# MLP up-projection of an encoder trunk: from channel-major matmuls of 512 and 256 columns to token-major matmuls of 512, its output turned on VectorE and GpSimd

## The chip, the cores and the metric

The kernel runs on one core of a Trainium2 chip. A core has TensorE (PE, matrix products into PSUM), ScalarE (ACT), VectorE (DVE), GpSimd (POOL) and SyncE (SP, which issues the weight DMAs here). Each engine takes its own queue of instructions in order. The metric is the time of one execution on the device in microseconds; three executions of the kernel before gave 2285.25, 2285.56 and 2286.99 us.

## The reference

Two layers of an encoder over 256 tokens of width 2048, all in float32. Layer 0 mixes by grouped-query attention, layer 1 by dilated windows; each is followed by a gated MLP with a depthwise convolution of width 3 over the tokens. The change touches the MLP alone:

```python
def rms_norm(x, gain):
    xf = x.astype(jnp.float32)
    y = xf * lax.rsqrt(jnp.mean(xf * xf, axis=-1, keepdims=True) + EPS) * gain.astype(jnp.float32)
    return y.astype(x.dtype)

def conv_ffn(h, w_up, conv_w, conv_b, w_down):
    u = h @ w_up                                  # (256, 2048) @ (2048, 11264)
    c = u.shape[-1]
    pad = CONV_WIDTH // 2
    u = lax.conv_general_dilated(u, conv_w[:, None, :].astype(u.dtype), window_strides=(1,),
                                 padding=((pad, pad),), dimension_numbers=('NWC', 'WIO', 'NWC'),
                                 feature_group_count=c) + conv_b
    gate, val = jnp.split(u, 2, axis=-1)
    return (jax.nn.silu(gate) * val) @ w_down

def reference(x, ...):
    h = x
    for i in range(DEPTH):                        # DEPTH = 2
        hn = rms_norm(h, mix_norm[i])
        ...
        h = h + conv_ffn(rms_norm(h, ffn_norm[i]), w_up[i], conv_w[i], conv_b[i], w_down[i])
    return rms_norm(h, final_norm)
```

## The kernel before

**Products.** A float32 product is made of three: each operand is split into a high part rounded to fp32r and a low rest, and high x high, high x low and low x high are summed in PSUM. The activations are split once per stage. Weights are split as they arrive: SP loads 128 x 1024 values (`raw`), ACT copies them rounded (`wh`, L113 and L165), DVE subtracts (`wl`, L114 and L166). `raw`, `wh` and `wl` have four buffers each (NRAW, NHL), so a new split waits until PE is done with the one four before it. The splits are recorded with a raised priority (AHEAD), so the scheduler puts them ahead of other work of the same engine.

**Token-major and channel-major.** In `feed` and `project` the stationary operand is a block of 128 tokens and the moving one 512 weight columns: two accumulators, one for each block of tokens, hold tokens on partitions and channels along the row (L153 to L155, 24 matmuls of 512 columns for each group of 512 input channels, "k-group"). The mixers' projections, the attention outputs and the down-projection go that way. The up-projection goes through `feed_T` instead: the stationary operand is 128 weight columns, the moving one the tokens, so channels lie on partitions. Its high weights meet high and low activations side by side in one matmul of 2 x 256 columns (L129); its low weights meet the high activations in one of 256 columns (L127). The halves of an accumulator must then be added (L428, L429), and the normalising factor `rstd` of each token, which lies along the row in this layout, is spread over the partitions once per layer by `bcast_rstd` (L375) and multiplied in (L431).

**The MLP.** 11264 columns are 11 gate blocks and 11 value blocks of 512, taken as pairs; pairs 0 to 5 and then 6 to 10 (HALVES). Each half makes its up-projections, and then a down-projection over its share of the hidden channels. Before, a block is taken in two halves of 256 columns (`hh`). The first one of a layer is fed in three parts, because the activations of the last k-group are still being turned and split at that time. `up_post` handles an accumulated half-block: empty it into `u`, make the middle tap and the bias of the convolution on ACT (L433), add the two outer taps on DVE (L438, L440); for the gate Silu on ACT (L443), for the value `glu`: the product on POOL (L448) and its split into `slots` for the down-projection (L242, L243).

**What sets the order.** Such work is written as generators: `start` runs one up to its first `yield`, and each `step`, called between groups of matmuls, runs the oldest one further; `drain` finishes what is left. The scheduler then orders each engine's queue by what its instructions need and by priority. The transposes of the activations between stages (`late_transpose`) already use DVE's blockwise transposes of 32 x 32 (`quad_T`, L288) and POOL copies between partitions (`quad_move`, L292), as does mixer B.

Of the kernel before, what the change touches and what calls it, by code (L numbers as in the profile page):

```python
# [13 lines left out]
P = 128  # L14
D = 2048
NT = 256
# [14 lines left out]
def tile_encoder(ctx: ExitStack, tc: tile.TileContext, x, xT, w_a, w_ao, q_gain, k_gain, w_b, w_bo,  # L31
# [26 lines left out]
    def nm(s):  # L58
        uid[0] += 1
        return f"{s}_{uid[0]}"  # L60
# [38 lines left out]

    def feed_T(acc, lhs, w, n, hh, kgs, first, last):  # L100
        raws = []
        for kg in kgs:
            raw = spool.tile([P, 2, 512], F32, tag="raw", name=nm("raw"), bufs=NRAW)
            raws.append(raw.rearrange("p a c -> p (a c)").rearrange("p (k c) -> p k c", c=NT))
            src = w[n, kg].rearrange("p (k c) -> p k c", c=512)[:, :, hh * NT:(hh + 1) * NT]
            nc.sync.dma_start(raws[-1], src)
        hls = []
        for rk in raws:
            wh = spool.tile([P, 2, 512], F32R, tag="wh", name=nm("wh"), bufs=NHL)
            wl = spool.tile([P, 2, 512], F32R, tag="wl", name=nm("wl"), bufs=NHL)  # L110
            wh, wl = (t.rearrange("p a c -> p (a c)").rearrange("p (k c) -> p k c", c=NT) for t in (wh, wl))
            with tc.high_priority(offset=AHEAD):
                nc.scalar.activation(wh, rk, AF.Copy)  # L113
                nc.vector.tensor_tensor(wl, rk, wh.bitcast(F32), ALU.subtract)  # L114
            hls.append((wh, wl))
        lows = (True, False) if kgs[0] == 2 and len(kgs) == 2 or kgs[0] == 3 else (False, True)
        spent, left, total = 0, len(kgs), 3 * len(kgs) * 8
        for n_run, low in enumerate(lows):
            fin = last and n_run == 1
            order = [(i, kt, j) for i in range(len(kgs)) for kt in range(4) for j in range(2)]  # L120
            for i, kt, j in sorted(order, key=lambda o: o[2]) if fin else order:
                c = slice(j * P, (j + 1) * P)
                st = first and n_run == 0 and i == 0 and kt == 0
                sp = fin and i == len(kgs) - 1 and kt == 3
                x, w2 = lhs[4 * kgs[i] + kt], hls[i]
                if low:
                    nc.tensor.matmul(acc[j][:, :NT], w2[1][:, kt, c], x[0], start=st, stop=sp)  # L127
                else:
                    nc.tensor.matmul(acc[j], w2[0][:, kt, c], x[2], start=st, stop=sp)  # L129
                spent += 1 if low else 2  # L130
                if spent >= total - 24 * (left - 1):
                    left -= 1
                    step()
# [234 lines left out]
    def bcast_rstd(rbc, rstd, pool):  # L368
        yield
        dg = pool.tile([P, 2, P], F32, name=nm("dg"))  # L370
        for m in range(2):
            nc.vector.tensor_scalar(dg[:, m, :], ident, rstd[:, m:m + 1], None, op0=ALU.mult)
        yield
        t = ps_tile()
        nc.tensor.matmul(t[:, :NT], ones, dg.rearrange("p m c -> p (m c)"), start=True, stop=True)  # L375
        nc.vector.tensor_copy(rbc, t[:, :NT])

# [16 lines left out]

    def ffn(l, hT, ss_in, cw, g_next, last, side=None):
        with tc.tile_pool(name=nm("fpool"), bufs=1) as fp:
            junk = junk_of(fp)
            next_space[0] = fp, ("quad", 1), ("tT", 1)
# [22 lines left out]
            def up_post(acc, n, hh, c, after=None):  # L421
                u = us.pop(0)
                us.append(u)
                k0 = 2 * hh
                yield
                v = fp.tile([P, 2, NT], F32, tag="v", name=nm("v"), bufs=2)
                for j in range(2):
                    nc.scalar.activation(v[:, j], acc[j][:, NT:], AF.Copy)  # L428
                    nc.vector.tensor_tensor(v[:, j], acc[j][:, :NT], v[:, j], ALU.add)  # L429
                o = u.rearrange("p j (m t) -> p j m t", m=2)[:, :, :, :P]  # L430
                nc.vector.tensor_tensor(o, v.rearrange("p j (m t) -> p j m t", m=2), rb4, ALU.mult)  # L431
                for j in range(2):
                    nc.scalar.activation(halves(c[:, j]), halves(u[:, j])[:, :, :P], AF.Identity,  # L433
                                         bias=tap(n, k0 + j, 3), scale=tap(n, k0 + j, 1))
                yield
                for j in range(2):
                    cj = halves(c[:, j])
                    nc.vector.scalar_tensor_tensor(cj, halves(u[:, j, :NT])[:, ::-1], tap(n, k0 + j, 0), cj,  # L438
                                                   ALU.mult, ALU.add)
# [626 lines left out]
```

## Time and profile before

| | |
|---|---|
| median of three runs | 2285.56 us |
| profiled execution | 2286.25 us |
| its span, first to last instruction | 2284.4 us |
| mean granted TensorE clock | 0.999 |
| PE / PEld / DVE / ACT / POOL busy | 2271.6 / 1941.1 / 1618.5 / 1199.2 / 202.4 us |
| HBM read | 429.2 MB, 189 GB/s over the span |

The profile shows one execution. Its views, as they are used below: the page gives each engine's busy time and, followed back from the last instruction, the chain of work that ended last; the groups put instructions of one line, engine and shape together, with their count, the time that they cover, the mean ns of one, and the idle time of the engine just before them with what ended it; a source or tile view gives min, median and max of one line's instructions; windows give busy time and counts of each engine in a stretch; the timeline gives instructions in order. Matmuls overlap in their pipeline, so the distance from one to the next is shorter than the length that is recorded for one.

### The profile page before, as it was taken

Reading aid. Unit: us, or ns where it says so; the run is one execution under the profiler, and the core shown is the slowest. Engines: PE = TensorE matmul, PEld = TensorE weight load, DVE = VectorE, ACT = ScalarE, POOL = GpSimd, SP = SyncE. Lnnn points to the kernel's source line nnn. Section 1 sums busy time; section 2 is a strip of 40 time slices with the busy share of each in tenths; the row PEclk is TensorE's granted clock in tenths of the full one; section 3 lists DMA queues with packets and bytes.
Section 4 is the critical chain, followed back from the end, with each engine's and each line's share of the span. In section 5 each row is a group of like instructions: output and inputs, shape, how many; then the busy total and the mean of one; then the engine's idle time right before and its main releaser. Section 6 shows DMA issues by size and latency. Waiting matters only on the chain.

```text
span 2284.4 us, 31068 instructions
## 1 busy us (share of the span) xinstructions
PE 2271.6 (99%) x11589; PEld 1941.1 (85%) x11589; DVE 1618.5 (71%) x2292; ACT 1199.2 (52%) x1755; POOL 202.4 (9%) x233
## 2 busy tenths in 40 slices
PE   9999999999999999999999999999999999999998
PEld 7888888888888888888888888888888888888887
DVE  6877977776457776878876876677777744677755
ACT  7565565554345554555454554446555533555543
POOL 2331100000000000010030003001000000000010
PEclk9999999999999999999999999999999999999999
DMA  8534565566555655576555554566565565555564
GB/s 301 167 131 163 196 192 186 185 195 196 194 190 184 192 189 199 184 217 206 190 178 180 181 186 167 182 199 206 186 194 188 190 196 192 190 189 192 185 199 152
DMA packets 256728, 433.43 MB, mean 190 GB/s; under 512 B 13752, under 2 KB 194744, under 8 KB 256448
## 3 DMA queue, kind: packets, MB, share of 16 engines
q1 hardware_dynamic: 254768, 425.91, 57.0%
q0 software_dynamic: 1520, 5.25, 1.1%
q8 instruction: 90, 1.47, 0.3%
q14 instruction: 62, 0.51, 0.1%
q10 hardware_dynamic: 288, 0.30, 0.0%
HBM read 429.20 MB, written 2.20 MB: 189 GB/s over the span
## 4 chain that ended last, share of the span: by engine, by line
PE 91%; DVE 4%; issue 1%; DMA 1%; ACT 1%; POOL 1%; SPq 0%; DVEq 0%; POOLq 0%; ACTq 0%
PE acc L129 27%; PE acc L154 15%; PE acc L155 15%; PE acc L153 15%; PE acc L127 14%; DVE wl L166 2%; DVE tT L297 2%; DMA raw<-in_w_b_dram 1%; PE ps L258 1%; PE ps L257 0%; PE ps L256 0%; ACT wh L165 0%; POOL wide L292 0%; PE ps L776 0%; PE ps L254 0%
## 5 line engine op out<-in xcount | busy, mean ns | idle before, releaser
L166 DVE TENSOR_TENSOR wl<-raw,wh 128x1024 fp32r<-128x1024 f32 (+1 forms) x452 | 549.9, 1220 | 305.0 <-ACT wh L165 301.5
L165 ACT ACTIVATE wh<-raw 128x1024 fp32r<-128x1024 f32 (+1 forms) x452 | 470.3, 1045 | 495.5 <-PE acc L155 408.2
L129 PE MATMUL acc<-xh,wh 128*128 128x512 f32 x2816 | 657.4, 390 | 1.2 <-DVE v L429 1.2
L129 PEld LDWEIGHTS acc<-xh,wh 128*128 128x128 f32 x2816 | 522.5, 188 | 106.5 <-DVE v L429 1.9
L114 DVE TENSOR_TENSOR wl<-raw,wh 128x1024 fp32r<-128x1024 f32 x352 | 416.7, 1223 | 83.7 <-ACT wh L113 78.1
L113 ACT ACTIVATE wh<-raw 128x1024 fp32r<-128x1024 f32 x352 | 362.8, 1054 | 64.9 <-ACT v L428 30.2
L153 PE MATMUL acc<-wh,ah 128*128 128x512 f32 x1008 | 392.7, 390 | 0.0
L155 PE MATMUL acc<-wh,al 128*128 128x512 f32 x1008 | 392.3, 389 | 0.0
L154 PE MATMUL acc<-wl,ah 128*128 128x512 f32 x1008 | 392.3, 389 | 0.0
L127 PEld LDWEIGHTS acc<-xh,wl 128*128 128x128 f32 x2816 | 350.6, 192 | 7.9 <-ACT wh L113 0.3
L127 PE MATMUL acc<-xh,wl 128*128 128x256 f32 x2816 | 353.2, 283 | 0.0
L153 PE MATMUL acc<-wh,xh 128*128 128x512 f32 x768 | 302.1, 394 | 1.0 <-ACT wh L165 1.0
L154 PE MATMUL acc<-wl,xh 128*128 128x512 f32 x768 | 299.5, 390 | 0.2 <-DVE wl L166 0.2
L155 PE MATMUL acc<-wh,xh 128*128 128x512 f32 x768 | 299.7, 390 | 0.0
L155 PEld LDWEIGHTS acc<-wh,al 128*128 128x128 f32 x1008 | 189.2, 188 | 39.2
L153 PEld LDWEIGHTS acc<-wh,ah 128*128 128x128 f32 x1008 | 189.3, 188 | 38.9
L154 PEld LDWEIGHTS acc<-wl,ah 128*128 128x128 f32 x1008 | 189.2, 188 | 38.9
L155 PEld LDWEIGHTS acc<-wh,xh 128*128 128x128 f32 x768 | 144.1, 188 | 30.6
L153 PEld LDWEIGHTS acc<-wh,xh 128*128 128x128 f32 x768 | 144.4, 188 | 29.1 <-ACT wh L165 1.4
L154 PEld LDWEIGHTS acc<-wl,xh 128*128 128x128 f32 x768 | 144.4, 188 | 28.4 <-DVE wl L166 0.5
L448 POOL TENSOR_TENSOR cv<-cg,cv 128x512 f32<-128x512 f32 x44 | 60.0, 1363 | 1153.6 <-DVE cv L440 1153.6
L242 ACT ACTIVATE ah<-cv 128x256 fp32r<-128x256 f32 x88 | 32.0, 411 | 169.2 <-POOL cv L448 169.2
(179 smaller groups left out, 1508.0 us busy)
## 6 DMA issues: line engine op xcount, KB each, us to landing
raw<-in_w_up_dram SPq DMA_DIRECT2D x352, 512.0 KB, 4.6
raw<-in_w_down_dram SPq DMA_DIRECT2D x176, 512.0 KB, 3.8
raw<-in_w_b_dram SPq DMA_DIRECT2D x144, 512.0 KB, 4.1
raw<-in_w_bo_dram SPq DMA_DIRECT2D x48, 512.0 KB, 3.6
raw<-in_w_a_dram SPq DMA_DIRECT2D x40, 512.0 KB, 4.3
raw<-in_w_ao_dram SPq DMA_DIRECT2D x32, 512.0 KB, 3.6
raw<-in_w_a_dram SPq DMA_DIRECT2D x16, 256.0 KB, 5.8
h<-in_x_dram SPq DMA_DIRECT2D x4, 512.0 KB, 7.8
```

The lines of the kernel that those rows point to most:

```text
L113: nc.scalar.activation(wh, rk, AF.Copy)
L114: nc.vector.tensor_tensor(wl, rk, wh.bitcast(F32), ALU.subtract)
L127: nc.tensor.matmul(acc[j][:, :NT], w2[1][:, kt, c], x[0], start=st, stop=sp)
L129: nc.tensor.matmul(acc[j], w2[0][:, kt, c], x[2], start=st, stop=sp)
L153: nc.tensor.matmul(accs[m], xh[:, c], wh[:, j, :], start=st, stop=False)
L154: nc.tensor.matmul(accs[m], xh[:, c], wl[:, j, :], start=False, stop=False)
L155: nc.tensor.matmul(accs[m], xl[:, c], wh[:, j, :], start=False, stop=sp)
L165: nc.scalar.activation(wh[:, c], r[:, c], AF.Copy)
L166: nc.vector.tensor_tensor(wl[:, c], r[:, c], wh[:, c].bitcast(F32), ALU.subtract)
L242: nc.scalar.activation(hi, src, AF.Copy)
L297: nc.vector.transpose(o[cols].rearrange("p a (m t) -> p a m t", m=2)[:, :, :, rows], s[rows].rearrange("p m (a c) -> p a m c", c=P)[:, :, ...
L448: nc.gpsimd.tensor_tensor(cv, cg, cv, ALU.mult)
```

## The change

The up-projection uses `project` and `project2` as the other projections do, with accumulators of 128 tokens x 512 channels. ACT empties them with `rstd` as the scale of each partition (`evac_scaled`). Then `turned` brings the block to channel-major: two DVE instructions transpose it in 32 x 32 blocks into `quad`, and 16 POOL copies move the blocks to their partitions in `u`, which now holds four groups of 128 channels. The convolution, Silu, product and split work on whole blocks of 512 channels. `feed_T`, `bcast_rstd`, `up_post` and `glu` are gone; new generators spread the work over the feeds, and the outputs of a value block are split while the next pair runs, or, for the last of a half, by `flush` in the down-projection.

```diff
-    def feed_T(acc, lhs, w, n, hh, kgs, first, last):
...
-    def bcast_rstd(rbc, rstd, pool):
...
+    def evac_scaled(pool, accs, rstd, bufs=2):
+        o = pool.tile([P, 2, 512], F32, tag="stg", name=nm("stg"), bufs=bufs)
+        for m in range(2):
+            nc.scalar.activation(o[:, m, :], accs[m], AF.Copy, scale=rstd[:, m:m + 1])
+        return o
...
-            next_space[0] = fp, ("quad", 1), ("tT", 1)
+            next_space[0] = fp, ("quad", 2), ("tT", 1)
...
-            us = [fp.tile([P, 2, 258], F32, name=nm("u")) for _ in range(3)]
+            us = [fp.tile([P, 4, 2, 129], F32, name=nm("u")) for _ in range(3)]
             for u in us:
-                nc.gpsimd.memset(u[:, :, P:P + 1], 0.0)
-            rbc = fp.tile([P, NT], F32, name=nm("rbc"))
-            rb4 = rbc.rearrange("p (m t) -> p m t", m=2)[:, None].to_broadcast([P, 2, 2, P])
-            start(bcast_rstd(rbc, rstd, fp))
+                nc.gpsimd.memset(u[:, :, 0, P:], 0.0)
...
-            def up_post(acc, n, hh, c, after=None):
...
-            def glu(cg, cv, slots, k0):
...
+            def conv(blk):
+                n, u, c = blk
+                for j in range(4):
+                    tc.keep_in_program_order(nc.scalar.activation(
+                        halves(c[:, j]), u[:, j, :, :P], AF.Identity, bias=tap(n, j, 3), scale=tap(n, j, 1)))
+                    if j == 1:
+                        yield
+                flat = u.rearrange("p j m t -> p j (m t)")
+                for j in range(4):
+                    cj = halves(c[:, j])
+                    for i, o in ((0, 0), (2, 1)):
+                        nc.vector.scalar_tensor_tensor(cj, halves(flat[:, j, o:o + NT])[:, ::-1], tap(n, j, i), cj,
+                                                       ALU.mult, ALU.add)
+                    if j == 1:
+                        yield
+
+            def turned(s, u):
+                quad = quad_tile(fp, "quad", 2)
+                for m in range(2):
+                    quad_T(quad, slice(m, 8, 2), s[:, m])
+                for q, c in QC:
+                    nc.gpsimd.tensor_copy(u[32 * c:32 * c + 32, :, :, 32 * q:32 * q + 32],
+                                          quad[32 * q:32 * q + 32, c].rearrange("p (j m) t -> p j m t", m=2))
+
+            def gate_gen(accs, blk, value):
+                s = evac_scaled(fp, accs, rstd, 1)
+                yield
+                if value is None:
+                    turned(s, blk[1])
+                    return
+                yield from product(value)
+                with tc.issue_after(value[4].pop()):
+                    turned(s, blk[1])
+
+            def product(value):
+                n, u, cv, cg, made, _, _ = value
+                yield from conv((n, u, cv))
+                made.append(nc.gpsimd.tensor_tensor(cv, cg, cv, ALU.mult).ins)
+
+            def value_gen(accs, blk, gate, last):
+                s = evac_scaled(fp, accs, rstd, 1)
+                yield
+                turned(s, blk[1])
+                for _ in range(1 if last else 4):
+                    yield
+                yield from conv(gate)
+                nc.scalar.activation(gate[2], gate[2], AF.Silu)
+                if last is not None:
+                    yield
+                    yield from act_split(last)
+
+            def act_split(value):
...
+                    tc.keep_in_program_order(nc.scalar.activation(hi, cv[:, j, :], AF.Copy))
+                    nc.vector.tensor_tensor(lo, cv[:, j, :], hi.bitcast(F32), ALU.subtract)
...
+            def flush(value):
+                yield
+                yield from product(value)
+                yield
+                yield
+                yield from act_split(value)
...
-                    for hh in range(2):
...
+                    if p == 0:
+                        va = project2(w_up[l], 0, NPAIR, hT, kgs, 1, gate_done)
+                    else:
+                        gate_done(project(w_up[l], p, hT, kgs))
+                        va = project(w_up[l], NPAIR + p, hT, kgs)
+                    start(value_gen(va, value, gate, last_value))
+                    last_value = value
...
+                start(flush(last_value))
...
-                drain(1)
```

The order of the instructions moves as follows.

On PE, in the up-projection of layer 0 before the change, at a pair's middle (`xh` are activations, `wl` and `wh` weights, the shape is that of the moving operand):

```order
L127 MATMUL acc_4601<-xh_2757,wl_4671 128x256
L127 MATMUL acc_4602<-xh_2757,wl_4671 128x256
L129 MATMUL acc_4601<-xh_2531,wh_4666 128x512
L129 MATMUL acc_4601<-xh_2534,wh_4666 128x512
L129 MATMUL acc_4601<-xh_2537,wh_4666 128x512
```

And on PE in the changed kernel, at the start of a value block of layer 0:

```order
L118 MATMUL acc_3939<-wh_3945,xh_2285 128x512
L119 MATMUL acc_3939<-wl_3946,xh_2285 128x512
L120 MATMUL acc_3939<-wh_3945,xh_2285 128x512
L118 MATMUL acc_3940<-wh_3945,xh_2285 128x512
L119 MATMUL acc_3940<-wl_3946,xh_2285 128x512
```

The runs of 256 columns are gone; all matmuls have 512, three for each accumulator.

On POOL, at the start of layer 0's MLP before the change (`rb`, `oh`, `rh`, `rl` belong to the bias lines of mixer B):

```order
L808 TENSOR_TENSOR rl<-rb,rh 128x24
L448 TENSOR_TENSOR cv_2624<-cg_2623,cv_2624 128x512
L448 TENSOR_TENSOR cv_2841<-cg_2840,cv_2841 128x512
L448 TENSOR_TENSOR cv_3066<-cg_3065,cv_3066 128x512
L448 TENSOR_TENSOR cv_3278<-cg_3277,cv_3278 128x512
```

And at the same place in the changed kernel:

```order
L792 TENSOR_TENSOR rl<-rb,rh 128x24
L400 COPY u_2609<-quad_2924 32x8x32 x16
L400 COPY u_2610<-quad_2994 32x8x32 x16
L416 TENSOR_TENSOR cv_2623<-cg_2622,cv_2623 128x1024
L400 COPY u_2608<-quad_3224 32x8x32 x16
```

In front of each product there now stand 32 copies, 16 for the gate and 16 for the value; the product covers 512 channels at once.

On ACT, in the middle of layer 0's first half before the change (`v` empties a half-block, `wh` splits weights, `cv` is the convolution's first step for a value, `ah` an output's split):

```order
L428 ACTIVATE v_3763<-acc_3501 128x256
L113 ACTIVATE wh_3800<-raw_3796 128x1024
L113 ACTIVATE wh_3804<-raw_3798 128x1024
L428 ACTIVATE v_3763<-acc_3502 128x256
L113 ACTIVATE wh_3850<-raw_3846 128x1024
L113 ACTIVATE wh_3854<-raw_3848 128x1024
L433 ACTIVATE cv_3498<-u_2608,cw_588 128x256 x2
```

And on ACT in the changed kernel, right behind the two instructions that empty the value block of layer 0's fourth pair (`stg_4117`), up to the convolution of that block:

```order
L130 ACTIVATE wh_4215<-raw_4191 128x1024
L130 ACTIVATE wh_4240<-raw_4236 128x1024
L425 ACTIVATE cg_3748<-cg_3748 128x1024
L435 ACTIVATE ah_3334<-cv_3343 128x256
L435 ACTIVATE ah_3336<-cv_3343 128x256
L130 ACTIVATE wh_4260<-raw_4238 128x1024
L435 ACTIVATE ah_3338<-cv_3343 128x256
L435 ACTIVATE ah_3340<-cv_3343 128x256
L130 ACTIVATE wh_4284<-raw_4280 128x1024
L130 ACTIVATE wh_4300<-raw_4282 128x1024
L130 ACTIVATE wh_4325<-raw_4321 128x1024
L382 ACTIVATE cv_3749<-u_2610,cw_588 128x256 x2
```

Six weight splits stand between the emptying of a value block and its convolution; the gate's convolution stands seven splits behind its block's emptying, and at a layer's start the two blocks' emptying and convolutions lie closer together.

More of the change, by code (lines that the diff above doesn't have):

```diff
@@ L98, in drain @@
             step()
-    def feed_T(acc, lhs, w, n, hh, kgs, first, last):
[L101 to L133, printed above, removed]
     def feed(accs, lhs, kg, wap, first, last, by_m=False, pieces=1, mid=None):
@@ L366, in junk_of @@
         return lambda: pool.tile([P, 512], F32, tag="junk", name=nm("junk"))
-    def bcast_rstd(rbc, rstd, pool):
[L369 to L376, printed above, removed]
     def load_taps(l):
@@ L418, in halves @@
             def halves(v):
                 return v.rearrange("p (m t) -> p m t", m=2)
-            def up_post(acc, n, hh, c, after=None):
-                u = us.pop(0)
-                us.append(u)
-                k0 = 2 * hh
-                yield
[L426 to L434, printed above, removed]
-                yield
[L436 to L439, printed above, removed]
-                    nc.vector.scalar_tensor_tensor(cj, halves(u[:, j, 1:NT + 1])[:, ::-1], tap(n, k0 + j, 2), cj,
-                                                   ALU.mult, ALU.add)
-                if after is None:
-                    nc.scalar.activation(c, c, AF.Silu)
-                else:
-                    yield from after()
@@ L583, in out_proj @@
         return hTn, ss
-    def evac_scaled(pool, accs, rstd, bufs=2):
-        o = pool.tile([P, 2, 512], F32, tag="stg", name=nm("stg"), bufs=bufs)
-        for m in range(2):
-            nc.scalar.activation(o[:, m, :], accs[m], AF.Copy, scale=rstd[:, m:m + 1])
-        return o
     def evac_split(pool, accs, rstd, whole=False):
```

41 lines of the change are left out of this document (16 added, 25 removed).

## The prediction, made before the run

> **What bounds the kernel now.** I read the page first, for the busy shares and the chain that ended last.
>
> ```profile
> span 2284.4 us, 31068 instructions
> PE 2271.6 (99%) x11589; PEld 1941.1 (85%) x11589; DVE 1618.5 (71%) x2292; ACT 1199.2 (52%) x1755; POOL 202.4 (9%) x233
> PE 91%; DVE 4%; issue 1%; DMA 1%; ACT 1%; POOL 1%; SPq 0%; DVEq 0%; POOLq 0%; ACTq 0%
> ```
>
> TensorE (PE) is busy for 99% of the span and makes 91% of the chain. So the question is how many matmuls there are, at what distance from one another, and whether PE is ever left waiting. What VectorE (DVE), ScalarE (ACT) or GpSimd (POOL) gain or lose counts only where it reaches PE.
>
> Next come the stages, in windows cut at the first matmul of each: the four up-projection halves, and behind them, for comparison, the first down-projection.
>
> ```profile
> 261.25:531.11 269.86, 268.62 (x1544) 1.00 0.61 193
> 661.67:883.94 222.27, 222.27 (x1282) 1.00 0.59 189
> 1547.69:1814.98 267.29, 267.29 (x1539) 1.00 0.60 193
> 1945.54:2167.81 222.27, 222.27 (x1282) 1.00 0.59 190
> 531.11:661.67 130.56, 130.56 (x578) 1.00 0.59 194
> ```
>
> The columns are the length, PE's busy time and count, the granted clock, the DMA share and GB/s. The up-projection takes 269.86 + 222.27 + 267.29 + 222.27 = 981.7 us, nearly without a hole, at full clock, with the DMA queues at 0.6. The last row gives the price of the other layout: this down-projection has 4 blocks x 6 k-groups x 24 = 576 matmuls of 512 columns (the window counts two more at its edges), so 130.56 / 576 = **226.67 ns** from one to the next.
>
> The chain of waits gives the rhythm inside the up-projection:
>
> ```profile
> 505.39 7.28 PE acc L129 x32
> 512.67 3.83 PE acc L127 x32
> 516.50 7.28 PE acc L129 x32
> ```
>
> 32 matmuls of 512 columns (L129) take 7.28 us, 227.5 ns each. 32 of 256 columns (L127) take 3.83 us, 119.7 ns each, although half of 226.67 would be 113.3. The narrow ones cost 6.3 ns more than their columns: each matmul has a fixed part, and the kernel has many short ones.
>
> **The change, part by part.** *Matmuls.* A unit of 32 + 32 is 11.11 us, and there are 2816 / 32 = 88 units:
>
> ```profile
> L129 PE MATMUL acc<-xh,wh 128*128 128x512 f32 x2816 | 657.4, 390 | 1.2 <-DVE v L429 1.2
> L127 PE MATMUL acc<-xh,wl 128*128 128x256 f32 x2816 | 353.2, 283 | 0.0
> L153 PE MATMUL acc<-wh,xh 128*128 128x512 f32 x768 | 302.1, 394 | 1.0 <-ACT wh L165 1.0
> ```
>
> (A mean here is a matmul's modelled length; the distances come from the chain.) 88 x 11.11 = 977.7 us. The change computes the same products as 22 blocks x 2 layers x 4 k-groups x 24 = 4224 matmuls of 512 columns, in the form of L153, which the mixers' projections already run. 4224 x 226.67 = 957.4 us. That is **-20.3 us**, all on PE's path.
>
> At this point the Trainium skill speaks against so much. The page "TensorE: Matmul & The Clock Gate", section "Back-to-back issue gap", gives a single matmul N/2.4 + 2.5 ns, so a fixed part of only 2.5 ns; 1408 matmuls fewer would then be an estimated 3.5 us. The rows here do not agree (226.67 and 119.7 ns, against 215.8 and 109.2 by the formula).
>
> *Start of each up-projection.* The two first halves are longer than their 24 units (266.6 us) by 3.2 and 0.7 us.
>
> ```profile
> 285.76 3.70 PE L129 MATMUL acc<-xh,wh 128*128 128x512 f32 x15 [1.24 <-DVE v L429]
> L375 PE MATMUL ps<-dg,ones x4: 377/379/381, 277.9 to 1564.6; 128*128 128x256 f32 x4
> ```
>
> In layer 0 PE waits 1.24 us for the DVE add that empties an accumulator (L429), and both starts hold two matmuls that spread rstd (L375). Both go. The four bias matmuls of layer 0 stay, 4 x 0.227 = 0.9 us. So 3.2 + 0.7 - 0.9 = 3.0 us can go here. New blocks are twice as long, so the first accumulators are wanted back later; what is late next is the POOL chain below.
>
> *ACT and DVE.* Per pair of column blocks (one gate, one value, 16 half-feeds of 12 x 226.67 = 2.72 us, 43.5 us):
>
> ```profile
> 400.00:443.50 43.50, 43.50 (x253) 38.60 (x252) 31.77 (x48) 24.47 (x38) 2.58 (x2) 1.00 0.61 194
> L429 DVE TENSOR_TENSOR v<-acc,v 128x256 f32<-128x256 f32 x176 | 73.7, 420 | 49.5 <-ACT v L428 49.5
> L428 ACT ACTIVATE v<-acc 128x256 f32<-128x256 f32 x176 | 64.5, 367 | 16.8 <-PE acc L129 16.8
> L431 DVE TENSOR_TENSOR u<-v,rbc 128x512 f32<-128x512 f32 x88 | 60.9, 692 | 2.9
> L588 ACT ACTIVATE stg<-acc,rstd 128x512 f32<-128x512 f32 x34 | 22.8, 685 | 8.1 <-PE acc L155 8.1
> L288 DVE STREAM_TRANSPOSE quad<-h 128x512 f32<-128x512 f32 x6 | 3.9, 694 | 0.4 <-ACT junk L278 0.2
> ```
>
> DVE loses 8 x 0.420 + 4 x 0.692 = 6.1 us and gains 4 transposes of 0.694 = 2.8; ACT loses 8 x 0.367 = 2.9 and gains 4 x 0.685 = 2.7. DVE goes from 31.8 to some 28.5 us of 43.5, ACT stays near 24.3. Neither is on the path, so this counts as nothing; cover gone would mean over 43.5 us of work.
>
> *POOL.* Per pair it now makes 32 copies of 32x256 and the same multiply (2 x 1.36 us). The copies exist in this trace:
>
> ```profile
> L292 POOL COPY wide<-quad x85: 388/398/1426, 268.7 to 1555.3; 32x256 f32<-32x256 f32 x85
> 1176.83 1.30 POOL L292 COPY wide<-quad 32x256 f32<-32x256 f32 x1
> 1176.70 1.18 DVE L166 TENSOR_TENSOR wl<-raw,wh 128x1024 fp32r<-128x1024 f32 x1
> 1166.50 20.96 POOL L292 COPY wide<-quad 32x256 f32<-32x256 f32 x32 [9.36 <-DVE quad L288]
> 1166.50:1187.50 21.00, 21.00 (x107) 17.70 (x106) 16.30 (x26) 9.64 (x15) 19.62 (x32) 1.00 0.53 175
> ```
>
> A copy takes 0.40 us, or 1.30 when it meets a weight split `wl` on DVE: it then ends just after the split. The Trainium skill has this as a rule (page "SBUF — State Buffer", section "Who interferes with whom"): a DVE instruction with two SBUF inputs and a GpSimd instruction that reads SBUF exclude one another; the trace agrees (1.30 against 0.40 us).
>
> Bounds for one copy, its gap of 0.04 included: 0.43 and 1.47 us. In the window of 32 copies the distance was 20.96 / 32 = 0.655 us, so about a quarter were held, with DVE busy 16.30 of 21.0 us. In the up-projection more of DVE's work has two SBUF inputs:
>
> ```profile
> L166 DVE TENSOR_TENSOR wl<-raw,wh 128x1024 fp32r<-128x1024 f32 x436 | 538.8, 1239 | 300.4 <-ACT wh L165 297.1
> L438 DVE SCALAR_TENSOR_TENSOR cg<-u,cw,cg 128x256 f32<-128x256 f32 x88 | 42.3, 483 | 28.2 <-ACT cg L433 28.2
> L165 ACT ACTIVATE wh<-raw 128x1024 fp32r<-128x1024 f32 x436 | 460.7, 1061 | 491.9 <-PE acc L155 408.2 <-issue 52.5 <-DMA raw<-in_w_b_dram 15.1
> ```
>
> I take a third held, 0.40 + 0.33 x 0.90 + 0.04 = **0.74 us**, near the measured mean; 16 copies are 11.8 us.
>
> *What waits for POOL.* The convolution's first step on ACT reads the turned tile, and the weight splits `wh` queue behind it. From the order: between a value block's evacuation and its convolution stand six splits, and a split runs when PE frees its buffer, so the sixth starts five half-feeds, 13.6 us, after the evacuation begins, and the convolution stands at the head at 14.7 us. The tile is ready at 1.4 (evacuation) + 1.4 (two transposes) + 11.8 = 14.6 us. That just meets. If it is late, PE notices only beyond the splits' own slack: a buffer is refilled three half-feeds (8.2 us) ahead of use, and `wh` + `wl` take 1.06 + 1.24, so 5.9 us are spare. The gate's tile has seven splits, and is behind the multiply.
>
> At a layer's start it is tighter: gate and value block end 5.4 us apart. ACT reaches the gate's convolution at 9.2 us, its tile comes at 14.6 (waits 5.4); the value's comes at 26.4 against 20.2 (waits 6.2). With 5.9 spare PE loses little; I take 1 us in each layer, bounds 0 (copies of 0.43) to some 25 (copies of 1.47).
>
> *End of a half.* The last pair's tail (turn, convolution, multiply, split; some 35 us) lies beside the down-projection's early k-groups, 10 or 8 feeds of 5.44 us, 54 or 43.5 us: nothing.
>
> **Sum.** 957.4 + 0.9 + 2 = 960.3 against 981.7: -21.4 us. The profiled execution took 2286.25 us (its span 2284.4 and 1.85 around it), so 2264.9; it lies 0.7 above the median of the three runs, 2285.56, which gives 2264.2. I say **2265.0**, its own range 2262 (no stall at all, counted from the median) to 2269 (3 us at each start).
>
> **Rivals.** *A, late tiles at the layer starts.* Were a copy 1.0 us, the gate's tile would come at 18.8 us (9.6 late, 3.7 beyond the slack), the value's at 34.8 (another 5.0): 8.7 us per layer, 17.4 in place of 2, so **2280**. For it: the queues are in order, and the start has no room to spare. Against it: the measured 0.655.
>
> *B, no gain in the rhythm.* If the extra of a short matmul were not a cost per matmul but came from the swap of weights, which both layouts make for every matmul, units would stay at 11.11 us and only a little of the start would be won: **2283 to 2285**. The skill's 2.5 ns would land near it, at an estimated 2282. Against it: the 226.67 ns are measured, in the very form that the change uses.
>
> *C, slower: POOL becomes the bound.* Its loop for a pair is 32 copies, the multiply (2.7), the gate's transposes (1.4), and the convolution on ACT and DVE (about 6, from four steps of each and a split between): 10 + 32c. It exceeds 43.5 us from **c = 1.05 us** on. If copies are held as often as DVE is busy, 31.77 / 43.5 = 73%, then c = 0.40 + 0.73 x 0.90 + 0.04 = 1.10, the loop is 45.1, and 18 of the pairs pay 1.6 us: +29, with A's 15 on top 2265 + 44 = **2309**. Against it: at DVE busy 78% of the quoted window only a quarter were held, since a waiting copy gets in between two DVE instructions.
>
> **How the numbers follow.** Forecast 66%, A 17%, B 6%, C 11%. The range 2262 to 2280 takes the forecast and A up to its 2280, some 80%. Under 0.2% (4.6 us) a measurement of this kernel cannot tell from no change. Faster by more: the forecast and most of A, 0.81; same: B and the end of A, 0.08; slower: C, 0.11.
>
> **What would show it.** In the new profile the four up windows should be near 263, 218, 262 and 218 us, the chain in steps of 0.23 us without holes; 704 more POOL copies, mean near 0.7 us; ACT waiting for POOL's copies by at most some 6 us at a time, mostly at the two layer starts. A mean above 1.0, or PE waiting for `wh` or `wl` in every pair, would make the prediction wrong; so would a distance of other than 227 ns.

## The result, and the profile after

The changed kernel takes **2262.76 us** (median of four runs, 2262.59 to 2263.00) against 2286.14 us for the kernel before beside it. The ratio is 0.9897, 95% interval 0.9885 to 0.9909: faster by 1.0%, beyond what a measurement of this kernel leaves open. The forecast was 2265.0, in a range of 2262 to 2280.

The page of the profile after, its span, engines and chain:

```profile
span 2261.1 us, 28533 instructions
PE 2250.5 (100%) x10177; PEld 1867.1 (83%) x10177; DVE 1593.0 (70%) x2110; ACT 1209.4 (53%) x1645; POOL 699.9 (31%) x915
PE 98%; DVE 1%; issue 0%; POOL 0%; ACT 0%; DMA 0%; SPq 0%; POOLq 0%; DVEq 0%; ACTq 0%
```

PE's busy time has fallen by 21.1 us and its instructions by 1412, that is the 1408 matmuls and the four that spread rstd. POOL works 497.5 us more, and it makes 0% of the chain.

The windows of the kernel after, cut at the first matmul of the four up-projection halves, with the first down-projection in front of the second half (length, PE busy and count, clock, DMA share, GB/s):

```profile
261.72:524.20 262.48, 262.44 (x1158) 1.00 0.60 199
524.20:654.76 130.56, 130.56 (x578) 1.00 0.56 194
654.76:872.36 217.60, 217.60 (x962) 1.00 0.58 193
```

In a window over all engines, the two halves of layer 1 (here after the length come PE, PEld, DVE, ACT and POOL busy):

```profile
1535.24:1796.35 261.11, 261.11 (x1153) 216.21 (x1152) 184.10 (x232) 153.88 (x199) 145.34 (x193) 1.00 0.60 198
1926.91:2144.51 217.60, 217.60 (x961) 180.18 (x960) 147.15 (x181) 122.13 (x151) 113.05 (x148) 1.00 0.58 194
```

The four sum to 958.8 us, against 981.7 before: -22.9 of the -23.3 us between the two profiled executions. The second halves are 960 matmuls in 217.60 us, 226.67 ns each, without one hole; layer 1's first half is 1152 in 261.11, also without one. Only layer 0's first half has more, 262.48: 0.9 for the bias matmuls and some 0.3 at its very first low weights, which come late (the second and third matmul start 0.42 and 0.34 us behind the one before, in place of 0.23). The first down-projection has not changed by a hundredth.

### The profile page after: what moved, and what is told of

It reads as the page before. It is cut to its first block, busy times and chain, and to the rows that moved or that the text cites. A ratio compares the mean times of both kernels' runs of the same rounds, so it can differ in the third digit from the quotient of the medians.

```text
span 2261.1 us, 28533 instructions
## 1 busy us (share of the span) xinstructions
PE 2250.5 (100%) x10177; PEld 1867.1 (83%) x10177; DVE 1593.0 (70%) x2110; ACT 1209.4 (53%) x1645; POOL 699.9 (31%) x915
## 4 chain that ended last, share of the span: by engine, by line
PE 98%; DVE 1%; issue 0%; POOL 0%; ACT 0%; DMA 0%; SPq 0%; POOLq 0%; DVEq 0%; ACTq 0%
PE acc L119 31%; PE acc L120 31%; PE acc L118 31%; PE ps L222 1%; PE ps L221 1%; PE ps L223 1%; PE ps L760 0%; PE ps L219 0%; PE ps L939 0%; DVE wl L131 0%; DVE tT L262 0%; DMA raw<-in_w_a_dram 0%; POOL t L692 0%; PE ps L923 0%; PE ps L589 0%
## 5 line engine op out<-in xcount | busy, mean ns | idle before, releaser
L131 DVE TENSOR_TENSOR wl<-raw,wh 128x1024 fp32r<-128x1024 f32 (+1 forms) x804 | 1008.4, 1258 | 551.4 <-ACT wh L130 548.3
L130 ACT ACTIVATE wh<-raw 128x1024 fp32r<-128x1024 f32 (+1 forms) x804 | 841.3, 1051 | 839.4 <-PE acc L120 728.9
L118 PE MATMUL acc<-wh,xh 128*128 128x512 f32 x2176 | 849.9, 391 | 0.6 <-ACT wh L130 0.6
L119 PE MATMUL acc<-wl,xh 128*128 128x512 f32 x2176 | 847.7, 390 | 0.3 <-DVE wl L131 0.2
L120 PE MATMUL acc<-wh,xh 128*128 128x512 f32 x2176 | 847.5, 389 | 0.0
L400 POOL COPY u<-quad 32x256 f32<-32x256 f32 x704 | 489.4, 695 | 540.1 <-DVE quad L253 512.3
L120 PEld LDWEIGHTS acc<-wh,xh 128*128 128x128 f32 x2176 | 408.4, 188 | 85.8
L119 PEld LDWEIGHTS acc<-wl,xh 128*128 128x128 f32 x2176 | 408.6, 188 | 84.2 <-DVE wl L131 1.7
L118 PEld LDWEIGHTS acc<-wh,xh 128*128 128x128 f32 x2176 | 408.6, 188 | 83.8 <-ACT wh L130 1.0
L353 ACT ACTIVATE stg<-acc,rstd 128x512 f32<-128x512 f32 x122 | 82.6, 686 | 31.6 <-PE acc L120 31.6
L390 DVE SCALAR_TENSOR_TENSOR cg<-u,cw,cg 128x256 f32<-128x256 f32 x176 | 82.2, 511 | 4.5 <-ACT cg L382 4.5
L390 DVE SCALAR_TENSOR_TENSOR cv<-u,cw,cv 128x256 f32<-128x256 f32 x176 | 74.3, 479 | 15.5 <-ACT cv L382 15.3
```

What stands on the lines that cost most here:

```text
L118: nc.tensor.matmul(accs[m], xh[:, c], wh[:, j, :], start=st, stop=False)
L119: nc.tensor.matmul(accs[m], xh[:, c], wl[:, j, :], start=False, stop=False)
L120: nc.tensor.matmul(accs[m], xl[:, c], wh[:, j, :], start=False, stop=sp)
L130: nc.scalar.activation(wh[:, c], r[:, c], AF.Copy)
L131: nc.vector.tensor_tensor(wl[:, c], r[:, c], wh[:, c].bitcast(F32), ALU.subtract)
L353: nc.scalar.activation(o[:, m, :], accs[m], AF.Copy, scale=rstd[:, m:m + 1])
```

## The experiments

Each edit is one to the changed kernel unless it says otherwise.

**Is it the number of matmuls?** Every matmul of the up-projection is cut in two of 256 columns:

```diff
-                nc.tensor.matmul(accs[m], xh[:, c], wh[:, j, :], start=st, stop=False)
-                nc.tensor.matmul(accs[m], xh[:, c], wl[:, j, :], start=False, stop=False)
-                nc.tensor.matmul(accs[m], xl[:, c], wh[:, j, :], start=False, stop=sp)
+                n = 512 // cut[0]
+                for x, w_, a, z in ((xh, wh, st, False), (xh, wl, False, False), (xl, wh, False, sp)):
+                    for b in range(cut[0]):
+                        cols = slice(b * n, (b + 1) * n)
+                        nc.tensor.matmul(accs[m][:, cols], x[:, c], w_[:, j, cols], start=a and b == 0, stop=z and b == cut[0] - 1)
```

(`cut[0]` is 2 in the up-projection and 1 elsewhere.)

> The changed kernel, with every matmul of the up-projection cut into two of 256 columns: 8448 in place of 4224, same columns, same layout, same turning. Theory (each matmul has a fixed part of some 13 ns): 8448 x 119.7 ns = 1011 us in place of 957.4, so the four up windows sum to about 1012 (958.8 in the changed kernel), and the time is 2316, slower than the kernel before. Rival B (the extra came from the old layout, not from the number): a 256-column matmul takes 113.3 ns here, and the time stays within 2263 to 2268.

2318.84 us; ratio to before 1.0142 (1.0122 to 1.0163); the four up windows sum to 1014.9 us. Its second halves in the windows, that of layer 0 over all engines (PE, PEld, DVE, ACT, POOL busy):

```profile
1969.88:2200.27 230.39, 230.39 (x1922) 1.00 0.58 183
669.50:899.89 230.39, 230.39 (x1921) 230.39 (x1920) 150.17 (x182) 121.88 (x151) 106.55 (x148) 1.00 0.57 183
```

1920 matmuls in 230.39 us are 120.0 ns each, what a 256-column matmul took in the old layout (119.7), and 6.7 ns above half of 226.67. So the cost goes with the number of matmuls, not with the layout: rival B falls. The two widths give the line: 226.67 - 120.0 = 106.7 ns for 256 columns, and 13.3 ns on top for each matmul. 1408 matmuls fewer at 13.3 ns are 18.8 us, most of the gain.

What the 13.3 ns consist of is not shown. Every matmul here loads its own stationary tile (1920 loads beside 1921 matmuls), and with 256 columns PEld is busy for the whole window, so the matmul's own part and its load's cannot be told apart. Nor does the line go on to narrower matmuls: at 128 columns it gives 66.7 ns, but the transposes of the run that turns on PE, below, stand 109 ns apart:

```profile
491.32 1.03 PE L401 MATMUL ps<-ident,stg 128*128 128x128 f32 x8
```

(Eight in 1.03 us, of which the last one's length is 0.27.)

**Does the turning cost anything?** The transposes and copies are left out, and the convolution reads tiles of zeros:

```diff
-                nc.gpsimd.memset(u[:, :, 0, P:], 0.0)
+                nc.gpsimd.memset(u, 0.0)
...
             def turned(s, u):
+                return
```

> The changed kernel without the turning: the 88 DVE transposes and 704 POOL copies are left out, the convolution reads tiles of zeros, so the MLP's output is not the reference's. Theory (turning is hidden beside PE): 2262 to 2263.2, up windows within 1 us of 958.8. Rival (POOL's copies hold DVE or ACT enough to cost PE time): 2260 or less.

2263.40 us (2262.92 to 2264.05), 0.2 above the expected range and no less than with the turning, and its up windows sum to 958.77 us against 958.8. 704 copies and 88 transposes cost nothing where the change puts them.

**What would it cost on the path?** The turning by PE instead, evacuated by ACT:

```diff
-                for m in range(2):
-                    quad_T(quad, slice(m, 8, 2), s[:, m])
-                for q, c in QC:
-                    nc.gpsimd.tensor_copy(u[32 * c:32 * c + 32, :, :, 32 * q:32 * q + 32],
-                                          quad[32 * q:32 * q + 32, c].rearrange("p (j m) t -> p j m t", m=2))
+                for jj in range(2):
+                    t = ps_tile()
+                    for j in range(2):
+                        for m in range(2):
+                            i = 2 * jj + j
+                            nc.tensor.transpose(t[:, j * NT + m * P:j * NT + (m + 1) * P],
+                                                s[:, m, i * P:(i + 1) * P], ident)
+                    o = u[:, 2 * jj:2 * jj + 2, :, :P]
+                    nc.scalar.activation(o, t.rearrange("p (j m c) -> p j m c", j=2, m=2), AF.Copy)
```

> The changed kernel with the turning done by 8 TensorE transposes of 128x128 for each block and 2 ACT copies out of PSUM, in place of 2 DVE transposes and 16 POOL copies. Theory (PE is the bound, and only work off PE is free): 352 transposes at 110 to 117 ns are 39 to 41 us more, 2302 to 2304, above the kernel before. Rival (the turn's latency also costs now, and a short turn would win it back): below 2300.

2302.71 us, as expected, 1.0072 of the kernel before (1.0052 to 1.0092): slower than that kernel. The 352 transposes cost 40 us, some 113 ns each. Token-major matmuls alone are no gain; they pay because the turn lies on engines that had time.

**Is the longer cover at the start part of the gain?**

```diff
-                        va = project2(w_up[l], 0, NPAIR, hT, kgs, 1, gate_done)
+                        ga = new_acc()
+                        for kg in kgs:
+                            if kg == 3:
+                                drain()
+                            feed(ga, hT, kg, w_up[l][0, kg], kg == 0, kg == 3)
+                        gate_done(ga)
+                        va = project(w_up[l], NPAIR, hT, kgs)
```

> The changed kernel with the first pair of each layer fed as the others are: gate block whole, then value block, so that only three feeds (16.3 us) lie ahead of the last k-group in place of six (32.6 us). Theory (part of the gain at the start comes from the longer cover over the late activations): PE waits 0.5 to 2 us in each layer for the last activations, 2264 to 2267. Rival (the cover is not needed, the start's gain was the spread of rstd and the DVE add alone): 2262.5 to 2263.2.

2262.85 us (2262.77 to 2262.88): the theory missed. The first halves are 262.46 and 261.12 us, as before the edit. In this run's timeline of DVE the last activations end at 275.6 us (a line has start and length in us, what ran and how often; in brackets, the idle time before it and what ended it):

```profile
273.91 1.66 DVE L214 SCALAR_TENSOR_TENSOR xh<-wide,gain,xh 128x256 fp32r<-128x256 f32 x4
```

The last k-group is due at 261.5 + 16.3 = 277.8 us, so three feeds cover them already. So what the start gained is put down to the two things that left it, rstd's spread and the wait for the add behind the first accumulators; this is by elimination, as no run puts them back.

**How far is POOL from being the bound?** 4, 8 or 16 of the copies of each block are made twice (`QC + QC[:4]` and so on):

```diff
-                for q, c in QC:
+                for q, c in QC + QC[:4]:
```

> The changed kernel with 20 POOL copies for each block in place of 16 (four blocks copied twice). Loop theory (POOL's copies, the product and the convolution's latency follow one another: 10.6 + 0.735 x 40 = 40.0 us for a pair of 43.5): no loss in the middle, a few us at the starts, 2263 to 2272. Throughput rival (POOL costs only when its own busy time passes 43.5 us; here 32.6): 2263.

> The changed kernel with 24 POOL copies for each block. Loop theory: 10.6 + 0.735 x 48 = 45.9 us for a pair of 43.5, 2.4 x 18 = 43 us more and some at the starts, 2300 to 2320. Throughput rival: POOL busy 38.5 us of 43.5, no loss, 2263 to 2268.

> The changed kernel with 32 POOL copies for each block. Loop theory: 10.6 + 0.735 x 64 = 57.6 us for a pair of 43.5, 14.1 x 18 = 254 us more, 2500 to 2560. Throughput rival: POOL busy 50.2 us, 6.7 x 20 = 134 us more, near 2400.

| copies a block | time, us | ratio to before (95%) | pair to pair, layer 0's first half |
|---|---|---|---|
| 16 (the change) | 2262.76 | 0.9897 (0.9885 to 0.9909) | 43.5 us |
| 20 | 2300.62 | 1.0058 (1.0034 to 1.0082) | 44.4 us |
| 24 | 2375.66 | 1.0394 (1.0364 to 1.0425) | 48.05 us |
| 32 | 2531.59 | 1.1077 (1.1044 to 1.1109) | 55.5 us |

(The last column is the time from one product on POOL to the next, the median of five.) The throughput rival falls: with 24 copies POOL would be busy 38.5 of 43.5 us, yet each pair takes 48. The loop theory was right in kind, but it missed the times with 20 and with 24 copies: its pairs were 40.0 and 45.9 us, and 44.4 and 48.05 were measured. With 32 copies the time fell into its range, yet the pair was 55.5 us and not 57.6: there the price of a copy, 0.735 us, was too high, and it made up for a part that was missing. The missing part is in the timeline of POOL, here with 24 copies:

```profile
458.74 16.83 POOL L400 COPY u<-quad 32x256 f32<-32x256 f32 x24 [5.64 <-DVE quad L253]
480.90 3.23 POOL L416 TENSOR_TENSOR cv<-cg,cv 128x1024 f32<-128x1024 f32 x1 [5.33 <-DVE cv L390]
484.08 17.14 POOL L400 COPY u<-quad 32x256 f32<-32x256 f32 x24
```

Value's copies, the product, the next gate's copies. POOL is idle 5.33 us while the convolution runs on ACT and DVE, as the prediction had it (6). But it is idle 5.64 us more between a gate's copies and the value's, waiting for the transposes of the value block. With 32 copies the gap is the same:

```profile
430.32 20.53 POOL L400 COPY u<-quad 32x256 f32<-32x256 f32 x32 [5.13 <-DVE quad L253]
456.18 3.21 POOL L416 TENSOR_TENSOR cv<-cg,cv 128x1024 f32<-128x1024 f32 x1 [5.32 <-DVE cv L390]
```

(A small DMA issue shortens it once, to 5.13.) ACT's timeline with 24 copies shows why:

```profile
453.13 1.10 ACT L382 ACTIVATE cg<-u,cw 128x256 f32<-128x256 f32 x2 [6.20 <-POOL u L400]
454.13 1.04 ACT L130 ACTIVATE wh<-raw 128x1024 fp32r<-128x1024 f32 x1
455.08 1.08 ACT L382 ACTIVATE cg<-u,cw 128x256 f32<-128x256 f32 x2
456.06 1.24 ACT L353 ACTIVATE stg<-acc,rstd 128x512 f32<-128x512 f32 x2
```

The value block is emptied (`stg`) behind the gate's convolution in ACT's queue, and that convolution waits for the gate's copies. So the loop is 5.64 + 5.33 + 3.23 = 14.2 us and the copies. With 24: 14.2 + 16.83 + 17.14 = 48.2, and 48.05 measured. With 20, where two stretches of copies took 15.30 and 15.02 us, it is 44.5, and 44.4 measured.

With 20 copies the loss of 38 us lies elsewhere, in the windows of layer 0 (up, down, up, down):

```profile
262.42:529.37 266.95, 264.85 (x1158) 1.00 0.60 195
529.37:666.20 136.83, 132.72 (x578) 0.99 0.57 186
666.20:883.96 217.76, 217.76 (x962) 1.00 0.59 192
883.96:999.50 115.54, 111.61 (x482) 0.97 0.56 181
```

The second half hardly loses, 217.76 against 217.60; the first half, with the layer's start, loses 4.5 us, and 6.3 and 6.7 are lost just behind the halves, in the down-projection, where ACT's timeline has

```profile
548.83 2.08 ACT L382 ACTIVATE cv<-u,cw 128x256 f32<-128x256 f32 x4 [6.84 <-POOL u L400]
550.82 2.93 ACT L130 ACTIVATE wh<-raw 128x1024 fp32r<-128x1024 f32 x3
557.83 0.73 ACT L435 ACTIVATE ah<-cv 128x256 fp32r<-128x256 f32 x2 [4.08 <-POOL cv L416]
```

two waits in a row, with only three weight splits between them.

Not all of this loss is waiting. Behind the second half PE's timeline (one matmul between the first two lines is left out) and windows of the same stretch read

```profile
906.63 0.80 PE L118 MATMUL acc<-wh,ah 128*128 128x512 f32 x1 [3.47 <-ACT wh L130]
908.48 0.63 PE L120 MATMUL acc<-wh,al 128*128 128x512 f32 x1
908.91 0.63 PE L118 MATMUL acc<-wh,ah 128*128 128x512 f32 x1
903.00:905.00 2.00, 0.16 (x1) 1.00 0.00 0
905.00:912.00 7.00, 4.91 (x11) 0.51 0.30 98
912.00:917.00 5.00, 5.00 (x24) 1.00 0.55 195
```

While PE waits, the granted clock (the first figure behind PE's count) falls to half, and it stays there until 912 us: the matmuls behind the wait stand 0.43 us apart in place of 0.23. The four down stages have a clock of 0.99, 0.97, 0.98 and 0.96, where the change has 1.00 three times and then 0.99. Over their lengths (136.83, 115.54, 137.92 and 123.66 us) that is, as an estimate, 11 us of the 38. In the first half, where no wait is longer than 0.9 us, the clock stays at 1.00.

**Are the tails the place, or does the lateness come from the middle?** The tail later in the queue:

```diff
             def flush(value):
                 yield
+                yield
+                yield
                 yield from product(value)
+                yield
+                yield
                 yield
                 yield
                 yield from act_split(value)
```

> The run with 20 copies, and the tail of each half (flush) set two steps later before its convolution and two more before its splits, so that six weight splits in place of four stand ahead of the convolution and six in place of three ahead of the outputs' splits. Theory (with 20 copies the loss behind a half lies in ACT's queue, where the tail's convolution waits 6.8 us and its splits 4.1 us with weight splits behind them): the four down stages lose most of their 27 us, the time falls from 2300.6 to about 2275; the rest, at the starts, stays. Rival (POOL itself is late, wherever ACT stands): 2295 to 2301.

And, without that, the doubled copies in the middle pairs only (`more = 0 if n % NPAIR in (0, 5, 6, 10) else 4`):

> The changed kernel with 20 copies for each block of the middle pairs, 16 in the first and last pair of each half. Theory (40.0 us for a pair of 43.5 fits, so the loss of the run with 20 copies everywhere was made at the starts and tails of the halves): 2262.5 to 2266. Rival (the loss builds up in the middle of a half and only shows at its end): the time stays above 2285.

The late tail gives 2284.12 us (16.5 less), the middle alone 2269.82. Neither expectation was met in full. Without doubled copies in the first and last pairs 31 of the 38 us are gone, but 7 remain with those in the middle, and 2 us in each of layer 0's down stages with the late tail: at 44.4 us for a pair of 43.5 each one hands some lateness on.

**Is it the order in ACT's queue?** With 20 copies and the late tail, the gate's convolution is set behind the emptying of its value block:

```diff
+    emptied = [None]
+
...
-            nc.scalar.activation(o[:, m, :], accs[m], AF.Copy, scale=rstd[:, m:m + 1])
+            emptied[0] = nc.scalar.activation(o[:, m, :], accs[m], AF.Copy, scale=rstd[:, m:m + 1]).ins
...
-            def conv(blk):
+            def conv(blk, behind=None):
...
-                    tc.keep_in_program_order(nc.scalar.activation(
+                    with tc.issue_after(behind) if behind is not None else ExitStack():
+                        tc.keep_in_program_order(nc.scalar.activation(
...
                 s = evac_scaled(fp, accs, rstd, 1)
+                behind = emptied[0]
...
-                yield from conv(gate)
+                yield from conv(gate, behind)
```

> The run with 20 copies and the late tail, and the convolution of a gate set behind the emptying of its value block in ACT's queue. In the runs with more copies POOL stands idle for 5.64 us in every pair between the gate's and the value's copies. Theory (this gap is ACT's order: the value block is emptied only behind the gate's convolution, which itself waits for the gate's copies, so POOL's loop is 14.2 us and the copies; here 44.5, without the gap 38.9 for a pair of 43.5): the gap is gone in the middle of a half or no longer part of a closed loop, pairs are 43.4 us apart in place of 44.3, ACT's waits of 3 to 5 us for the gate's tile in every pair fall below 1 us, and the time falls from 2284.1 to 2268 to 2279, the rest lying at the starts. Rival (the copies and the DVE work that holds them fill the pair): 2282 or more, pairs 44 us apart.

**2266.99 us**, 1 us below the expected range: 17.1 us less than with the late tail alone. With both, the same 880 copies that cost 38 us cost 4, and the ratio to before is 0.9915 (0.9886 to 0.9944). Its timeline of POOL in the middle of a half:

```profile
440.82 15.30 POOL L403 COPY u<-quad 32x256 f32<-32x256 f32 x20 [4.36 <-DVE quad L253]
461.46 3.23 POOL L419 TENSOR_TENSOR cv<-cg,cv 128x1024 f32<-128x1024 f32 x1 [5.34 <-DVE cv L393]
464.64 15.34 POOL L403 COPY u<-quad 32x256 f32<-32x256 f32 x20
484.34 15.30 POOL L403 COPY u<-quad 32x256 f32<-32x256 f32 x20 [4.36 <-DVE quad L253]
504.98 3.23 POOL L419 TENSOR_TENSOR cv<-cg,cv 128x1024 f32<-128x1024 f32 x1 [5.34 <-DVE cv L393]
```

From product to product it is 43.52 us, the pace of PE. A gap is still there, 4.36 us, but POOL now waits for PE to finish the value block, not for its own gate copies, as the emptying on ACT ahead of the first of these lines shows:

```profile
438.64 1.37 ACT L355 ACTIVATE stg<-acc,rstd 128x512 f32<-128x512 f32 x2 [0.98 <-PE acc L120]
```

The rest, 1.8 us in each layer's first half, lies at the start, where 20 copies are late all the same. With 16 copies this order has nothing to win, since PE does not wait there; it was not run.

**Is it the buffers' slack that hides POOL?** Three buffers for split weights (`NRAW, NHL = 4, 3`):

> The changed kernel with three buffers for the split weights in place of four, in every stage. Theory (a late tile costs PE only beyond the slack that these buffers give, 5.9 us with four and 3.2 with three; ACT waited for POOL up to 3.8 and 4.1 us): the up windows grow by 1 to 10 us from 958.8, at the starts and ends of the halves, the middle of a half stays at 2.72 us a half-feed; other stages may grow too. Rival (the slack is not what hides POOL): up windows within 1 us of 958.8.

2291.03 us (ratio 1.0022, 1.0011 to 1.0033). The up windows sum to 962.2 us, 3.4 more, inside the expected range; in layer 0 the first half grows and the second stays whole:

```profile
274.17:538.14 263.97, 262.43 (x1157) 1.00 0.61 196
669.39:886.99 217.60, 217.60 (x961) 1.00 0.60 193
```

So the slack does hide something at the starts, 1.5 to 1.9 us in a layer. It is one hole in each, in layer 0 at

```profile
337.98 1.10 ACT L382 ACTIVATE cv<-u,cw 128x256 f32<-128x256 f32 x2 [2.39 <-POOL u L400]
343.29 2.39 POOL L416 TENSOR_TENSOR cv<-cg,cv 128x1024 f32<-128x1024 f32 x1 [5.34 <-DVE cv L390]
343.65 3.10 DVE L131 TENSOR_TENSOR wl<-raw,wh 128x1024 fp32r<-128x1024 f32 x1
346.81 0.50 PE L119 MATMUL acc<-wl,xh 128*128 128x512 f32 x1 [1.54 <-DVE wl L131]
```

The late copies alone do not make it. The weight split for which PE waits starts beside the product on POOL, takes 3.10 us and ends 1.07 us behind the product. At the 1.27 us that a split takes on average in the change it would have ended at 344.9 us, before PE's next matmul was due at 345.1. In the middle pairs such a split takes 3.10 us again (at 474.80, for one) and makes no hole, so the lateness at the start seems to be needed too; the two were not run apart. Most of the 28 us is lost in other stages, which is no evidence on the change.

## Why the prediction was right, point by point

*Matmuls, -20.3 us.* Right, and shown by the cut: the new distance is the 226.67 ns of the down-projection, and halves of 256 columns cost 120 ns each in the new layout as well.

*Start, -3.0 and +2 back.* The gain was there but 0.4 short of whole, and the 2 us for late tiles were not paid: of 960.3 us forecast for the four windows 958.8 came. ACT's waits for POOL's copies are (total us, times, longest):

```profile
ACT cv L382 <- POOL u L400: 19.8, 6, 3.8
ACT cg L382 <- POOL u L400: 6.1, 4, 2.9
```

At each layer's start these are 2.9 us for the gate's tile and 2.4 for the value's, not 5.4 and 6.2. The 6.2 was also counted wrongly: the first wait already sets ACT back, as rival A's working allows for, so 0.8 was left of it. Forecast on this count are 6.2 us in all, measured 5.3, below the 5.9 that the buffers spare, and PE did not wait. That term was mis-sized, and it makes 1.5 of the 2.2 us by which the time came out below the forecast; the rest is the step from the summed 2264.2 to 2265.0. The other 15.0 us of ACT's waits lie behind the four halves, 3.75 each, where the prediction looked for nothing; so its sign that they come mostly at the two layer starts did not hold. The longer cover over the late activations was no term of it, and the plain start shows that the cover earns nothing.

*ACT and DVE, nothing.* Right for PE, but DVE's load was put too low; the window of one pair (PE, PEld, DVE, ACT, POOL busy) is

```profile
400.00:443.50 43.50, 43.50 (x193) 36.02 (x192) 31.08 (x41) 25.64 (x34) 25.84 (x34) 1.00 0.59 194
```

DVE stands at 31.1 us, not 28.5: its weight splits (1.27 us each in this window, 1.22 before) and its outputs' splits (0.58 against 0.42) became longer, which is some 1.4 us of it, and a fifth output split falls in this window, 0.6 more; the rest was not followed up. PE waits for DVE nowhere in the up-projection for more than 0.2 us.

*POOL's copies, 0.74 us with the gap.* Right. The copies' row and two stretches of 16:

```profile
L400 POOL COPY u<-quad x704: 389/404/1493, 301.9 to 2157.3; 32x256 f32<-32x256 f32 x176
460.94 11.64 POOL L400 COPY u<-quad 32x256 f32<-32x256 f32 x16
482.55 12.29 POOL L400 COPY u<-quad 32x256 f32<-32x256 f32 x16 [9.97 <-DVE quad L253]
```

11.6 and 12.3 us for 16, against 11.8 forecast. A third of the copies held gave that; the copies' mean of 695 ns lies a third of the way from 0.40 to 1.30 us. The third itself was chosen, somewhere between a quarter and 73%, so there is luck in hitting it.

*End of a half, nothing.* Right in the sum, for the wrong reason. The early feeds of the down-projection cover the outputs, but the tight place is ACT's queue, in the kernel after as well:

```profile
537.42 2.08 ACT L382 ACTIVATE cv<-u,cw 128x256 f32<-128x256 f32 x4 [3.75 <-POOL u L400]
539.41 2.94 ACT L130 ACTIVATE wh<-raw 128x1024 fp32r<-128x1024 f32 x3
546.45 0.72 ACT L435 ACTIVATE ah<-cv 128x256 fp32r<-128x256 f32 x2 [4.10 <-POOL cv L416]
```

Four splits stand ahead of the tail's convolution, not six, and three ahead of the outputs' splits. Each of the two waits stays within the 5.9 us that the buffers spare, and PE does not wait; four more copies a block break it.

*Rivals.* B fell by the cut. A and C did not come, but the loop of C was priced wrongly: not 10 but 14.2 us and the copies, since the emptying of the value block stands behind the gate's convolution. It decides from a copy of about 0.92 us on, not 1.05. With the measured 0.75 the loop is 14.2 + 23.9 = 38.1 us of 43.5, so the change stood 5 us from its cliff and not 10, as the 44.4 us with 20 copies bear out.

## What to carry to other kernels

Where PE is the bound, count matmuls as well as columns: read the distance of the wide and of the narrow ones from the chain; what the narrow ones take beyond their share of the columns is what a wider tile saves. Work that is moved to an idle engine is free only while the queues that wait for it have room: look for what stands behind its reader in an in-order queue, above all an instruction that the same engine's next job depends on, because that closes a loop. Busy time does not show the margin: an engine at 59% of a pair (25.84 of 43.5 us) cost 38 us of PE's time with four more copies a block, and two changes of place in the queues around it, the tail set later and the gate's convolution behind the emptying, gave 16.5 and then 17.1 of them back. And price a wait on PE at more than its length: an estimated 11 of the 38 us were a lowered clock behind the waits.

## What the hardware showed that was not expected

More copies do not each cost the mean of one. A block's 16 took 11.6 to 12.3 us, 20 took 15.3, 24 took 17.1 and 32 took 20.8: the first four added cost some 0.8 us each, the next twelve 0.46, little above an unheld copy's 0.40 and its gap. Held copies (over 0.8 us) are 209 of 704 in the change and 264, 266 and 270 in the three runs with more, so from 20 on hardly another one was held. The weight splits that hold them are the same number in all these runs; that this sets the limit was not tested.

A copy hardly holds DVE in turn: the weight splits `wl` of 128x1024 take a mean of 1269 ns in the change and 1250 without the copies (the first line is the change, the second the run without turning):

```profile
L131 DVE TENSOR_TENSOR wl<-raw,wh 128x1024 fp32r<-128x1024 f32 x788 | 997.2, 1269 | 546.9 <-ACT wh L130 543.8
L131 DVE TENSOR_TENSOR wl<-raw,wh 128x1024 fp32r<-128x1024 f32 x788 | 983.3, 1250 | 666.4 <-ACT wh L130 663.2
```

POOL's product does hold DVE. Behind a half of the changed kernel a split that starts beside it takes 3.42 us and ends 1.08 behind it:

```profile
543.20 3.22 POOL L416 TENSOR_TENSOR cv<-cg,cv 128x1024 f32<-128x1024 f32 x1 [5.81 <-DVE cv L390]
544.08 3.42 DVE L131 TENSOR_TENSOR wl<-raw,wh 128x1024 fp32r<-128x1024 f32 x1
```

With four buffers PE does not notice this; with three, such a split stood in front of the hole shown above.
